# A Conformer macaron layer on one core: one more seven-product pair in each feed-forward group, four summed weight tiles a group, and the second feed-forward's two summed buffers exchanged

## The chip, the cores and the metric

The kernel runs on one core of a Trainium2 chip. The metric is the device time of one execution in microseconds, as the median of several runs. The core has a tensor engine (PE, with its weight loads shown as PEld), a vector engine (DVE), a scalar engine (ACT), GpSimd (POOL) and a sync engine (SP) that issues most of the transfers from HBM. Each engine works through its own list of instructions in a fixed order; an instruction whose inputs are not there waits, and so do those behind it on that engine.

## The reference, cut to what matters

```python
def swiglu_ffn(h, w_in, w_out):
    gate, up = jnp.split(h @ w_in, 2, axis=-1)
    return (jax.nn.silu(gate) * up) @ w_out

# per layer
h = rms_norm(x, ffn1_norm[l]);  x = x + 0.5 * swiglu_ffn(h, ffn1_w_in[l], ffn1_w_out[l])
...                             # convolution and gating mixers, output projection, cross-attention
h = rms_norm(x, ffn2_norm[l]);  x = x + 0.5 * swiglu_ffn(h, ffn2_w_in[l], ffn2_w_out[l])
return rms_norm(x, final_norm)
```

There are 256 tokens, the model's width is 2048 and the feed-forward's is 5632, so `w_in` is 2048 x 11264 and `w_out` 5632 x 2048, all in float32. The change touches the product with `ffn1_w_in` and, in one line, that with `ffn2_w_in`.

## The kernel before, in words

**Products in three parts.** A float32 number is split into a high part (ACT casts it, L397) and a low part (DVE subtracts the high part from it, L398). A product of two such numbers is high·high + high·low + low·high, three matrix products (`three`, L318 to L320; `by_two`, L331, L332 and L334). Each has a 128x128 stationary side and 512 columns. The weights pass through SBUF in tiles of 128 x 1024 (512 KB): SP loads the raw tile (L408), ACT makes its high part and DVE its low part, and PE uses both.

**Groups and pairs.** Each feed-forward's first product is done in 11 blocks j of 1024 columns (512 gate, 512 up). Block 0 is plain. In blocks 1 to 10, called groups, the 16 tiles k of a group are taken as 8 pairs, by the letters of PATTERNS. A "C" pair (`eight`) takes the eight products of two tiles as they are, 24 matrix products, and needs two splits. An "S" pair (`seven`) takes seven products of sums and differences, 21 matrix products; for it DVE makes the sums (L470, L471, L477, L484, 512 columns each) and three and a half tiles are split. The token side of an S pair is made once, by `sides`, beside block 0, into one of four places (`forms`), of which three are used.

**Summed tiles.** Some tiles of C pairs (SUMMED, k = 2, 7, 13) get their low part without DVE: SP loads the raw tile (L425), ACT writes its negative to the low half (L426) and its cast to the high half (L427), and POOL issues a transfer that loads the same weights again and adds them onto the low half (L428). There are two such buffers, `hl_s` and a part of `more` (in the second feed-forward `hl_s` and `hl_s2`), used by turns (`buffer`), with one raw tile each. The refill of a buffer is issued when the tile in it has been used (`following`): L426 then waits for the last product that reads the low half.

**The end of a group.** After the last S pair `joins_sevens` copies and adds sums (L521 on ACT, L522 to L525 on DVE); after the last pair DVE adds the remaining four banks (L550 four times), ACT takes the silu (L510) and DVE the product (L512). All eight PSUM banks are in use, so the first products of the next group wait for these adds.

**What sets the order.** The code is written in program order, and a scheduler at build time sorts the instructions onto the engines' lists; `issue_after` puts a part of the program behind a named instruction in that sorting. On the chip the lists are fixed. Raw tiles go round nine places (four of `wraw`, five of `spare`) less those given to summed tiles; split tiles go round three of `whl`, two of `ring` and one of `more`.

Of the kernel before, what the change touches and what calls it, by code (L numbers as in the profile page):

```python
# [2 lines left out]

# [1 line left out]

# [9 lines left out]
ALU = mybir.AluOpType  # L15
# [18 lines left out]
SCALE = float(HD) ** -0.5  # L34


PATTERNS = ("SCSCSCCC", "SCSCSCCC")

SUMMED = ((2, 7, 13), (2, 7, 13))
ALONE = (2, 10)  # L40


# [36 lines left out]
def layer(ctx: ExitStack, tc: tile.TileContext, a: dict):  # L79
    nc = tc.nc  # L80
    out = a["out"]
# [232 lines left out]
    NG = F // G  # L314
# [27 lines left out]
    class FeedForward:  # L342
# [4 lines left out]


        def __init__(self, stack, tags, x_hl, gain, w_in, pattern, summed, w_out=None, pair=False):
            self.w_out, self.out_forms = w_out, None  # L350
            self.x_hl, self.gain, self.w_in, self.pattern = x_hl, gain, w_in, pattern
            self.tags, self.pattern_sums = tags, summed
            self.spairs = [p for p, c in enumerate(pattern) if c == "S"]
            self.own = stack.enter_context(tc.tile_pool(name="own", bufs=1))
            self.low = ExitStack()
            low = self.low.enter_context(tc.tile_pool(name="h_low", bufs=1))
            self.high = ExitStack()
            high = self.high.enter_context(tc.tile_pool(name="h_high", bufs=1, side="right"))
# [12 lines left out]
            self.forms = [  # L371
                forms[:, i * 1024:(i + 1) * 1024].rearrange("p (f two n) -> p f two n", two=2, n=P) for i in range(4)
            ]
            spare = big.tile([P, 8192], F32, name="spare", tag=tags[2])
            self.x2 = spare[:, :4096].rearrange("p (t d) -> p t d", t=2)
            self.free = spare[:, 4096:]
            self.sums = spare[:, 4096:5120]
            self.raws = [spare[:, i * 1024:(i + 1) * 1024] for i in (5, 0, 1, 2, 3)]
            self.raw_at = 0

            self.raws_summed = [self.raws.pop()]
            self.u = [spare[:, 6144 + i * 512:6144 + (i + 1) * 512] for i in range(4)]
            self.at = 0
            self.next = None
            self.hA = self.hB = self.hC = None
            self.hls = [self.own.tile([P, 2, 1024], F32R, name="hl_s")]
            self.first = self.hls[0].rearrange("p a (f two n) -> p (a f) two n", f=2, two=2)
            if pair:
                self.hls.append(second)
                self.raws_summed.append(self.h[8].rearrange("p a b -> p (a b)"))  # L390
# [19 lines left out]

        def buffer(self, at):

            return at % 2 if not self.pair or self.sums_at[at][0] < 8 else 0

        def following(self, at):
            same = [i for i in range(at + 1, len(self.sums_at)) if self.buffer(i) == self.buffer(at)]
# [2 lines left out]
        def summed(self, at):  # L419

            if at >= len(self.sums_at):
                return
            j, k = self.sums_at[at]
            raw, hl = self.raws_summed[self.buffer(at)], self.hls[self.buffer(at)]
            nc.sync.dma_start(out=raw, in_=self.w_in[j, :, k])  # L425
            nc.scalar.activation(out=hl[:, 1], in_=raw, func=AF.Copy, scale=-1.0)  # L426
            nc.scalar.copy(out=hl[:, 0], in_=raw)  # L427
            nc.gpsimd.dma_start(out=hl[:, 1], in_=self.w_in[j, :, k], accum_op=ALU.add)  # L428
# [91 lines left out]
        def joins_sevens(self, b, p1, u2, u4, u5):  # L520
            nc.scalar.copy(out=p1, in_=b["1"])  # L521
            nc.vector.tensor_tensor(out=u2, in0=p1, in1=b["6"], op=ALU.add)  # L522
            nc.vector.tensor_tensor(out=u4, in0=u2, in1=b["5"], op=ALU.add)
            nc.vector.tensor_tensor(out=u2, in0=u2, in1=b["7"], op=ALU.add)
            nc.vector.tensor_tensor(out=u5, in0=u2, in1=b["5"], op=ALU.add)  # L525

        def group(self, j, r, after=()):
            if self.pair and j == NG - 2:
                both = self.high_pool.tile([P, 2, 2, G], F32, name="h_pair", tag="pair")
                self.h[NG - 2:] = [both[:, i] for i in range(2)]  # L530
            b = {}
            self.begun = set()
            self.banks(b, "57612348")
            after = list(after)
            p1, u2, u4, u5 = self.u
            n = len(self.pattern)
            for p, c in enumerate(self.pattern):
                if c == "S":
                    self.seven(j, p, b, p == self.spairs[-1])
                    if p == self.spairs[-1]:  # L540
                        self.joins_sevens(b, p1, u2, u4, u5)
                else:
                    late = p > self.spairs[-1] and len(after) > 0
                    self.eight(j, p, b, p == n - 1, late)
                    if p > self.spairs[-1] + 1:
                        for _ in range(2):
                            if after:
                                after.pop(0)()
            for acc, u in (("2", p1), ("4", u2), ("3", u4), ("8", u5)):
                nc.vector.tensor_tensor(out=u, in0=u, in1=b[acc], op=ALU.add)  # L550
            self.give(j, (p1, u2), (u4, u5), r)
# [58 lines left out]
        def run(self, before, after, root, more=None, early=False):  # L610
            acc = token_accs()
            sums = self.pattern_sums
            self.sums_at = [(j, k) for j in range(1, NG) for k in sums if j < NG - 1 or k < min(14, sums[-1])]
            if self.pair:

                self.sums_at = [at for at in self.sums_at if at[0] < 8] + [(j, k) for j in range(8, NG) for k in ALONE]
            for k in range(KD):
                if k == 0 and early:
                    w = self.early(before)
                else:  # L620
                    before(k)
# [68 lines left out]
    with ExitStack() as stack:  # L690
        ff = FeedForward(stack, ("S1", "S0", "S2"), x_hl, lambda k: gains[:, k:k + 1], a["ffn1_w_in"], PATTERNS[0], SUMMED[0], a["ffn1_w_out"])
# [6 lines left out]
        def x_more(k):  # L698
            if k == 6:
                nc.sync.dma_start(out=pv, in_=a["pv"])  # L700
            if k in (2, 4, 6, 8):
                x_squares(k // 2 - 1)
            if k in (6, 9, 12):
                ff.sides(k // 3 - 2)

        def x_root():
            nc.vector.tensor_tensor(out=r_x, in0=tot[:, 0], in1=tot[:, 1], op=ALU.add)
# [3 lines left out]
        def x_given():  # L711

            more = xt.tile([P, 4, 1024], F32R, name="more", tag="x")
            ff.ring.append(more[:, :2])
            ff.hls.append(more[:, 2:])
            ff.raws_summed.append(ff.raws.pop())

        turns = ff.run(x_arrives, x_more, x_root, x_given, early=True)

# [81 lines left out]
    with ExitStack() as stack:  # L801
        with tc.tile_pool(name="mix", bufs=1) as pool:
# [239 lines left out]
            at = [part for _, part in later].index(conv_swish_0)  # L1042
# [327 lines left out]
```

## Time and profile before

| | before |
|---|---|
| median of the runs, us | 2088.95 (2088.29 to 2089.9) |
| time of the profiled execution, us | 2088.91 |
| its span in the trace, us | 2087.1 |
| PE matrix products in the trace | 9765 |
| DVE, ACT, POOL instructions in the trace | 2302, 1470, 81 |
| HBM read, MB | 437.44 |

The span runs from the first to the last instruction in the trace. The time of an execution is 1.8 us longer, which lies around the span.

### The profile page before, as it was taken

How to read it: one execution, taken by the hardware profiler on the slowest of the kernel's cores; microseconds unless marked ns; L12 is line 12 of the kernel's file. 1: busy time of each engine (PE TensorE's matmuls, PEld its weight loads, DVE VectorE, ACT ScalarE, POOL GpSimd, SP SyncE). 2: the span in 40 equal slices, each digit the busy share in tenths (PEclk: the TensorE clock that was granted, in tenths of full speed). 3: DMA queues.
4: the chain of work that ended last, by engine and by line, in shares of the span. 5: the costliest groups of instructions: out<-in, count | busy, mean ns of one | idle time of the engine just before them, and what ended most of it. 6: DMA issues, size and time to landing. Idle time of an engine off the chain costs nothing.

```text
span 2087.1 us, 26730 instructions
## 1 busy us (share of the span) xinstructions
PE 2076.4 (99%) x9765; PEld 1739.0 (83%) x9765; DVE 1622.5 (78%) x2302; ACT 1174.4 (56%) x1470; POOL 66.0 (3%) x81
## 2 busy tenths in 40 slices
PE   9999999999999999999999999999999999999998
PEld 8888888888888888888888899888888888888886
DVE  7888888877777689989877666778888888787754
ACT  8665666555545554445764455566665655554443
POOL 0000000000000000000000000000000000000000
PEclk9999999999999999999999999999999999999999
DMA  9787778755566576655555543687777777556664
GB/s 366 246 263 246 232 223 263 230 182 192 188 203 234 180 238 199 186 179 187 180 196 192 184 160 124 200 291 224 237 236 253 222 217 230 169 166 203 195 192 152
DMA packets 122245, 441.30 MB, mean 211 GB/s; under 512 B 13569, under 2 KB 13953, under 8 KB 121729
## 3 DMA queue, kind: packets, MB, share of 16 engines
q1 hardware_dynamic: 113184, 407.08, 57.1%
q0 software_dynamic: 8352, 31.46, 8.1%
q8 instruction: 76, 1.25, 0.2%
q10 hardware_dynamic: 576, 1.06, 0.1%
q14 instruction: 57, 0.46, 0.1%
HBM read 437.44 MB, written 2.10 MB: 211 GB/s over the span
## 4 chain that ended last, share of the span: by engine, by line
PE 87%; issue 11%; POOL 1%; DMA 1%; ACT 0%; DVE 0%; DVEq 0%; POOLq 0%
PE acc L332 11%; PE acc L331 11%; PE acc L334 11%; PE acc L204 8%; PE acc L205 8%; PE acc L203 8%; PE acc L154 8%; PE acc L162 4%; PE acc L318 3%; PE acc L319 3%; PE acc L320 3%; PE aux L306 1%; PE aux L318 1%; PE aux L319 1%; PE aux L320 1%
## 5 line engine op out<-in xcount | busy, mean ns | idle before, releaser
L124 ACT CAST hl<-raw 128x1024 fp32r<-128x1024 f32 (+1 forms) x315 | 327.1, 1040 | 358.9 <-PE acc L205 191.9
L125 DVE TENSOR_TENSOR hl<-raw,hl 128x1024 fp32r<-128x1024 f32 (+1 forms) x315 | 381.2, 1212 | 165.0 <-ACT hl L124 163.6
L397 ACT CAST hl<-raw 128x1024 fp32r<-128x1024 f32 (+1 forms) x151 | 147.6, 988 | 117.3 <-PE acc L334 48.2
L398 DVE TENSOR_TENSOR hl<-raw,hl 128x1024 fp32r<-128x1024 f32 (+1 forms) x151 | 172.2, 1145 | 47.4 <-ACT hl L397 45.7
L398 DVE TENSOR_TENSOR hl<-spare,hl 128x1024 fp32r<-128x1024 f32 (+1 forms) x125 | 144.7, 1162 | 32.5 <-ACT hl L397 30.3
L397 ACT CAST hl<-spare 128x1024 fp32r<-128x1024 f32 (+1 forms) x125 | 124.3, 1002 | 66.4 <-PE acc L334 24.2
L332 PE MATMUL acc<-hl,x_hl 128*128 128x512 f32 x388 | 140.9, 390 | 0.1
L331 PE MATMUL acc<-hl,x_hl 128*128 128x512 f32 x388 | 135.7, 390 | 0.0
L334 PE MATMUL acc<-hl,x_hl 128*128 128x512 f32 x388 | 120.6, 390 | 0.0
L397 ACT CAST ring<-spare 128x1024 fp32r<-128x1024 f32 (+1 forms) x83 | 82.1, 993 | 59.6 <-issue 19.1
L398 DVE TENSOR_TENSOR ring<-spare,ring 128x1024 fp32r<-128x1024 f32 (+1 forms) x83 | 95.2, 1150 | 20.3 <-ACT ring L397 19.6
L332 PE MATMUL acc<-ring,x_hl 128*128 128x512 f32 x276 | 101.3, 389 | 0.0
L204 PE MATMUL acc<-hl,x_hl 128*128 128x512 f32 x256 | 100.7, 393 | 0.0
L204 PE MATMUL acc<-hl,m_hl 128*128 128x512 f32 x256 | 100.4, 392 | 0.0
L205 PE MATMUL acc<-hl,m_hl 128*128 128x512 f32 x256 | 100.3, 392 | 0.0
L205 PE MATMUL acc<-hl,x_hl 128*128 128x512 f32 x256 | 100.0, 391 | 0.0
L331 PE MATMUL acc<-ring,x_hl 128*128 128x512 f32 x276 | 98.6, 390 | 0.0
L203 PE MATMUL acc<-hl,m_hl 128*128 128x512 f32 x256 | 90.9, 392 | 0.0
L203 PE MATMUL acc<-hl,x_hl 128*128 128x512 f32 x256 | 90.2, 392 | 0.0
L334 PE MATMUL acc<-ring,x_hl 128*128 128x512 f32 x276 | 86.2, 389 | 0.0
L332 PEld LDWEIGHTS acc<-hl,x_hl 128*128 128x128 f32 x388 | 72.6, 188 | 15.5 <-DVE hl L133 0.4
L334 PEld LDWEIGHTS acc<-hl,x_hl 128*128 128x128 f32 x388 | 72.9, 188 | 15.1
(518 smaller groups left out, 5100.8 us busy)
## 6 DMA issues: line engine op xcount, KB each, us to landing
spare<-in_ffn_w_in SPq DMA_DIRECT2D x184, 512.0 KB, 6.8
raw<-in_ffn_w_in SPq DMA_DIRECT2D x157, 512.0 KB, 5.9
raw<-in_ffn_w_out SPq DMA_DIRECT2D x138, 512.0 KB, 4.0
hl_s<-in_ffn_w_in POOLq DMA_DIRECT2D x42, 512.0 KB, 8.3
raw<-in_w_mix_vg SPq DMA_DIRECT2D x32, 512.0 KB, 4.3
raw<-in_w_k SPq DMA_DIRECT2D x32, 512.0 KB, 3.6
raw<-in_w_v SPq DMA_DIRECT2D x32, 512.0 KB, 4.0
raw<-in_w_mix_out SPq DMA_DIRECT2D x32, 512.0 KB, 4.4
```

The lines of the kernel that those rows point to most:

```text
L124: nc.scalar.copy(out=hl[:, 0, :size], in_=raw[:, :size])
L125: newest[0] = nc.vector.tensor_tensor(out=hl[:, 1, :size], in0=raw[:, :size], in1=hl[:, 0, :size].bitcast(F32), op=ALU.subtract)
L154: done = nc.tensor.matmul(acc, lhsT=hi[:, k], rhs=xs[k], start=first and k == 0, stop=last and k == kk - 1, skip_group_check=True,)
L162: done = nc.tensor.matmul(acc[:, 0], lhsT=lo[:, k], rhs=xs[k][:, 0], start=False, stop=last and k == kk - 1, skip_group_check=True,)
L203: nc.tensor.matmul(acc[t], lhsT=x[:, 0, s], rhs=hi[:, k], start=k0 + k == 0, stop=False)
L204: nc.tensor.matmul(acc[t], lhsT=x[:, 0, s], rhs=lo[:, k], start=False, stop=False)
L205: nc.tensor.matmul(acc[t], lhsT=x[:, 1, s], rhs=hi[:, k], start=False, stop=k0 + k == nk - 1)
L331: nc.tensor.matmul(acc[t][g], lhsT=x[:, 0, s], rhs=hi[:, cols[g]], start=(t, g) in first, stop=False)
L332: nc.tensor.matmul(acc[t][g], lhsT=x[:, 0, s], rhs=lo[:, cols[g]], start=False, stop=False)
L334: nc.tensor.matmul(acc[t][g], lhsT=x[:, 1, s], rhs=hi[:, cols[g]], start=False, stop=last)
L397: self.cast = nc.scalar.copy(out=hl[:, 0, :n], in_=raw[:, :n])
L398: newest[0] = nc.vector.tensor_tensor(out=hl[:, 1, :n], in0=raw[:, :n], in1=hl[:, 0, :n].bitcast(F32), op=ALU.subtract)
```

## The change

In the first feed-forward, groups 1 to 9 take the pattern SCSCSCSC, with four S pairs; group 10 keeps SCSCSCCC. The summed tiles are k = 2, 6, 10 and 14 (in group 10 those below 13), so four a group instead of three, still in two buffers, but with three raw tiles by turns instead of two; the third is taken from the ring of raw tiles. `sides` is called four times in block 0 instead of three. The first S pair of a group is sorted in behind the last add of `joins_sevens` of the group before. In the second feed-forward the two summed buffers exchange their turns for j < 8, and what comes after stays in `hl_s`. Lines move by two to nine.

```diff
-PATTERNS = ("SCSCSCCC", "SCSCSCCC")
-SUMMED = ((2, 7, 13), (2, 7, 13))
+PATTERNS = ("SCSCSCSC", "SCSCSCCC")
+LAST = "SCSCSCCC"
+SUMMED = ((2, 6, 10, 14), (2, 7, 13))
...
         def buffer(self, at):
-            return at % 2 if not self.pair or self.sums_at[at][0] < 8 else 0
+            if self.pair:
+                return (at + 1) % 2 if self.sums_at[at][0] < 8 else 0
+            return at % 2
...
-            raw, hl = self.raws_summed[self.buffer(at)], self.hls[self.buffer(at)]
+            raw = self.raws_summed[self.buffer(at) if self.pair else at % len(self.raws_summed)]
+            hl = self.hls[self.buffer(at)]
...
-            nc.vector.tensor_tensor(out=u5, in0=u2, in1=b["5"], op=ALU.add)
+            self.joined = nc.vector.tensor_tensor(out=u5, in0=u2, in1=b["5"], op=ALU.add)
...
-            n = len(self.pattern)
-            for p, c in enumerate(self.pattern):
+            pattern = self.pattern if j < NG - 1 else LAST
+            n, done = len(pattern), pattern.rindex("S")
+            for p, c in enumerate(pattern):
                 if c == "S":
-                    self.seven(j, p, b, p == self.spairs[-1])
-                    if p == self.spairs[-1]:
+                    with nullcontext() if p or self.joined is None else tc.issue_after(self.joined.ins):
+                        self.seven(j, p, b, p == done)
+                    if p == done:
                         self.joins_sevens(b, p1, u2, u4, u5)
...
-            self.sums_at = [(j, k) for j in range(1, NG) for k in sums if j < NG - 1 or k < min(14, sums[-1])]
+            self.sums_at = [(j, k) for j in range(1, NG) for k in sums if j < NG - 1 or k < 13]
...
-            if k in (6, 9, 12):
-                ff.sides(k // 3 - 2)
+            if k in (4, 7, 10, 13):
+                ff.sides(k // 3 - 1)
...
-            ff.raws_summed.append(ff.raws.pop())
+            ff.raws_summed += [ff.raws.pop() for _ in range(2)]
```

Over the whole program PE has 9701 rows in its list where it had 9728, DVE 2353 for 2304, ACT 1487 for 1456 and POOL 96 for 86 (ten more adding transfers); SP has 788 in both. The rows below are from the lists: line, operation, out<-in, size. The number behind a name tells buffers apart; two names can be one place in turn.

**First place: from block 0 to group 1, on ACT.** `h0` is the result of block 0 (silu, L510 before, L516 now), `spare` and `raw` are raw tiles. Before:

```order
L397 CAST hl_471<-spare_132 128x1024
L397 CAST hl_526<-raw_505 128x1024
L397 CAST more_490<-raw_503 128x1024
L397 CAST ring_131<-spare_132 128x1024
L510 ACT_TABLE_LOAD
L510 ACTIVATE h0_120<-acc_134,r_x2_109 128x512
L397 CAST hl_536<-raw_505 128x512
L510 ACTIVATE h0_120<-acc_136,r_x2_109 128x512
```

Now, with the first S pair of group 1 in `hl_532`, `ring_131` (the sums) and `more_498`:

```order
L399 CAST ring_131<-spare_132 128x1024
L399 CAST hl_479<-spare_132 128x1024
L516 ACT_TABLE_LOAD
L516 ACTIVATE h0_120<-acc_134,r_x2_109 128x512
L516 ACTIVATE h0_120<-acc_136,r_x2_109 128x512
L399 CAST hl_532<-spare_132 128x1024
L399 CAST ring_131<-spare_132 128x1024
L399 CAST more_498<-spare_132 128x1024
L432 ACTIVATE more_498<-spare_132 128x1024
```

The three casts of the first S pair stood ahead of the table load and the two silu rows, and stand behind them. PE's list at this place now reads as follows; `acc_136` and `acc_137` are block 0's banks, and the L320 rows are the first products of group 1:

```order
L333 MATMUL acc_137<-hl_479,x_hl_108 128x512
L334 MATMUL acc_137<-hl_479,x_hl_108 128x512
L336 MATMUL acc_136<-hl_479,x_hl_108 128x512
L336 MATMUL acc_137<-hl_479,x_hl_108 128x512
L320 MATMUL acc_503<-ring_131 128x512
L320 MATMUL aux_504<-ring_131 128x512
L320 MATMUL aux_505<-more_498,ring_131 128x512
L320 MATMUL acc_506<-more_498,x_hl_108 128x512
```

The silu of `acc_136` follows the last but one row of block 0, and the first row of group 1 needs `ring_131`, two casts behind that silu.

**Second place: from group 2 to group 3, on ACT.** L521 (now L527) is the copy of `joins_sevens`; `h2` is the result of group 2. Before, the group's last refill of a summed tile (L426) stands at the end:

```order
L521 COPY spare_132<-acc_793 128x512
L397 CAST ring_131<-spare_132 128x1024
L397 CAST more_490<-spare_132 128x1024
L397 CAST hl_1099<-spare_132 128x1024
L397 CAST hl_1109<-raw_1093 128x1024
L397 CAST hl_1118<-raw_1095 128x1024
L426 ACTIVATE more_490<-spare_132 128x1024
```

Now:

```order
L527 COPY spare_132<-acc_808 128x512
L399 CAST ring_131<-spare_132 128x1024
L432 ACTIVATE more_498<-spare_132 128x1024
L433 CAST more_498<-spare_132 128x1024
L399 CAST hl_1121<-spare_132 128x1024
L399 CAST hl_1167<-raw_1165 128x1024
L399 CAST ring_131<-spare_132 128x1024
L516 ACTIVATE h2_122<-spare_132,r_x2_109 128x512
```

`hl_1121` is the sums' tile of group 3's first S pair and the `ring_131` below it the second one of that pair. They stood ahead of the refill and stand behind it. In PE's list the last row that reads the low half which L432 overwrites (an L334 row of tile k = 14) stands 14 rows ahead of the first row of group 3; the row that needs `hl_1121` is that first row, and the one that needs `ring_131` is two rows on.

**Third place: refills inside a group, on ACT.** This is group 3's refill of `hl_s` after k = 2 (for k = 10), in the list now:

```order
L399 CAST hl_1192<-spare_132 128x1024
L399 CAST hl_1202<-raw_1186 128x1024
L399 CAST ring_131<-raw_1188 128x1024
L399 CAST more_498<-raw_1237 128x1024
L432 ACTIVATE hl_s_133<-spare_132 128x1024
L433 CAST hl_s_133<-spare_132 128x1024
```

The two casts ahead of L432 wait for PE rows that stand four and two rows ahead of the one L432 waits for. From that row, the last that reads the old low half, to the first that needs the new one, PE's list has 41 rows. Counted in this way, the distances in groups 1 to 10 of the first feed-forward were 106 to 115 rows; now they are 40 to 81, and six of them are 40, 41, 41, 45, 40 and 41 rows (in groups 2, 3, 6, 6, 8 and 9; the 45 is that of `more`, the others are of `hl_s`). In the second feed-forward one distance was 43 rows and the others 72 and more; now the least is 72.

More of the change, by code (lines that the diff above doesn't have):

```diff
@@ L1 @@
 from collections import deque
-from contextlib import ExitStack
+from contextlib import ExitStack, nullcontext
 import numpy as np
@@ L383, in __init__ @@
             self.at = 0
-            self.next = None
+            self.next = self.joined = None
             self.hA = self.hB = self.hC = None
@@ L535, in group @@
             p1, u2, u4, u5 = self.u
-            n = len(self.pattern)
-            for p, c in enumerate(self.pattern):
+            pattern = self.pattern if j < NG - 1 else LAST
+            n, done = len(pattern), pattern.rindex("S")
+            for p, c in enumerate(pattern):
                 if c == "S":
-                    self.seven(j, p, b, p == self.spairs[-1])
-                    if p == self.spairs[-1]:
+                    with nullcontext() if p or self.joined is None else tc.issue_after(self.joined.ins):
+                        self.seven(j, p, b, p == done)
+                    if p == done:
                         self.joins_sevens(b, p1, u2, u4, u5)
                 else:
-                    late = p > self.spairs[-1] and len(after) > 0
+                    late = p > done and len(after) > 0
                     self.eight(j, p, b, p == n - 1, late)
-                    if p > self.spairs[-1] + 1:
+                    if p > done + 1:
                         for _ in range(2):
```

## The prediction

> **What bounds the kernel now.** I read the page first, then what PE waits for, then the stretches of one group, then the rows of single places. The page's head, busy line, PE clock by slices and chain:
>
> ```profile
> span 2087.1 us, 26730 instructions
> ...
> PE 2076.4 (99%) x9765; PEld 1739.0 (83%) x9765; DVE 1622.5 (78%) x2302; ACT 1174.4 (56%) x1470; POOL 66.0 (3%) x81
> ...
> PEclk9999999999999999999999999999999999999999
> ...
> PE 87%; issue 11%; POOL 1%; DMA 1%; ACT 0%; DVE 0%; DVEq 0%; POOLq 0%
> ```
>
> PE is busy 99% of the span at full clock, and the chain that ended last is made of PE rows. The view of PE's waits has two entries:
>
> ```profile
> PE aux L232 <- DVE ones L229: 1.1, 1, 1.1
> PE acc L332 <- DMA hl_s<-in_ffn_w_in: 0.8, 1, 0.8
> ```
>
> So a product less is time less, and each new wait of PE is time more. The second entry, in the second feed-forward, and the rows around it are the most useful of the trace. PE's timeline there, eleven microseconds earlier:
>
> ```profile
> 1695.75 0.39 PE L331 MATMUL acc<-hl_s,x_hl 128*128 128x512 f32 x1
> 1695.98 0.39 PE L332 MATMUL acc<-hl_s,x_hl 128*128 128x512 f32 x1
> 1696.20 0.39 PE L331 MATMUL acc<-hl_s,x_hl 128*128 128x512 f32 x1
> 1696.43 0.39 PE L332 MATMUL acc<-hl_s,x_hl 128*128 128x512 f32 x1
> ```
>
> The timelines of ACT and POOL:
>
> ```profile
> 1696.86 1.06 ACT L426 ACTIVATE hl_s<-spare 128x1024 fp32r<-128x1024 f32 x1 [1.21 <-PE acc L332]
> ...
> 1698.32 0.86 POOL L428 DMA_DIRECT2D hl_s<-in_ffn_w_in  x1 [27.69 <-ACT hl_s L426]
> ```
>
> The chain's piece, start and length:
>
> ```profile
> 1698.32 8.77 DMA hl_s<-in_ffn_w_in
> ```
>
> And PE's timeline at its end (in brackets the wait and what ended it):
>
> ```profile
> 1705.95 0.39 PE L331 MATMUL acc<-hl_s,x_hl 128*128 128x512 f32 x1
> 1707.13 0.50 PE L332 MATMUL acc<-hl_s,x_hl 128*128 128x512 f32 x1 [0.80 <-DMA hl_s<-in_ffn_w_in]
> 1707.47 0.39 PE L334 MATMUL acc<-hl_s,x_hl 128*128 128x512 f32 x1
> ```
>
> Three things are read from these rows. PE rows start every 0.227 us ((1696.43 - 1695.75) / 3), though each is shown as 0.39 long. A refill goes: last reader at 1696.43, ACT 0.43 later, POOL's transfer 1.46 after that, landing 8.77 later, PE 0.04 later, in all 10.70 us. And 43 rows were left for it, 9.75 us, so PE was held: 1705.95 to 1707.13 and then 0.34 where rows take 0.227, **1.07 us** too long. That is the one hold of PE in either feed-forward's groups.
>
> The stretches of block 0 and of two plain groups (columns: PE, PEld, DVE, ACT, POOL busy us and counts, clock, share of the DMA engines, GB/s):
>
> ```profile
> 5.00:46.00 41.00, 40.93 (x184) 33.64 (x183) 35.19 (x60) 35.33 (x56) 1.02 (x1) 1.00 1.03 392
> 131.00:172.00 41.00, 41.00 (x182) 33.99 (x181) 34.36 (x41) 24.84 (x28) 2.50 (x3) 1.00 0.76 244
> 214.00:255.00 41.00, 41.00 (x183) 33.96 (x182) 34.33 (x41) 25.56 (x29) 2.60 (x3) 1.00 0.78 244
> ```
>
> In a group PE has no gap, DVE 6.7 us to spare in 41 and ACT 16; shares of busy time alone would let the change pass. What decides is who stands behind whom.
>
> **The change part by part.** The sum starts from the profiled execution, 2088.91 us (span 2087.1, 1.8 around it), within 0.1 us of the median of the runs, 2088.95.
>
> *Removed.* PE's list has 27 rows less (three in each of nine groups): 27 x 0.227 = **-6.1 us**. The exchange of buffers in the second feed-forward takes the 43-row refill away; the least distance there is then 72 rows, 16.3 us, for a need of 10.7: **-1.07 us**. Free of all else the kernel would take 2081.7.
>
> *Added work.* DVE has 49 rows more, 5.4 a group; at the 0.69 to 1.22 us of its rows (shown below) that is 3.7 to 6.6 us a group on top of 34.4. The period is 4 x 21 + 4 x 24 = 180 PE rows, 40.8 us (183 before). It just fits, so as busy time I cost it at nothing; at the upper end it would be 0.2 us a group. The fourth `sides` stands in block 0, where DMA is full (1.03 of the engines) but DVE and ACT have 5.7 us: nothing, at most 0.5. The ring of raw tiles shrinks from seven to six places, for 12 loads a group where there were 13: a place comes round every 6 x 40.8 / 12 = 20.4 us instead of 7 x 41.5 / 13 = 22.3. Plain loads land in 6.2 (median, below), so I cost it at nothing.
>
> *First place, start of group 1.* ACT's rows there before, timeline:
>
> ```profile
> 47.99 1.28 ACT L510 ACT_TABLE_LOAD   x1
> 49.29 0.69 ACT L510 ACTIVATE h<-acc,r_x 128x512 f32<-128x512 f32 x1
> 49.87 0.61 ACT L397 CAST hl<-raw 128x512 fp32r<-128x512 f32 x1
> ...
> 50.96 1.05 ACT L397 CAST hl<-spare 128x1024 fp32r<-128x1024 f32 x1
> 51.91 1.05 ACT L397 CAST more<-spare 128x1024 fp32r<-128x1024 f32 x1
> ```
>
> A silu row holds ACT 0.58, a cast 0.95, and its result is there after 1.05. Now the second silu waits for PE's last but one row of block 0, 0.45 ahead of group 1. It starts at -0.45 + 0.43 = -0.02, the casts follow at 0.56, 1.51 and 2.46, and the third ends at 3.51. PE's third row of group 1, due at 0.45, needs it: 3.51 + 0.05 - 0.45 = **+3.1 us**. Before, these casts stood ahead of the silu and nothing was held. Bounds: if the raw tiles come late too (DMA is full there), 5; if they are early, 3.1 stays, since the silu sets it.
>
> *Second place, nine group starts.* L432 waits for the last reader of k = 14's low half, 12 to 15 rows ahead of the next group, and the casts of that group's first S pair stand behind it. From group 2 to 3: the reader at 0, L432 at 0.43, L433, two casts, and the third cast after four rows of 0.96 at 4.27, ready at 5.32 + 0.05; PE wants it 16 rows on, at 3.63: held 1.74. The nine starts have their own number of casts in between and of rows ahead; worked out in the same way they give 1.0, 1.7, 0.5, 1.3, 1.5, 0.7, 1.0, 1.7 and 0.5, together **+10.0 us**. In three of them DVE's subtraction for the low part is late as well, behind the adds L550, which end last here:
>
> ```profile
> 130.97 0.69 DVE L550 TENSOR_TENSOR spare<-spare,acc 128x512 f32<-128x512 f32 x1 [1.53 <-PE acc L334]
> 131.57 1.22 DVE L398 TENSOR_TENSOR ring<-raw,ring 128x1024 fp32r<-128x1024 f32 x1
> 132.71 1.88 DVE L550 TENSOR_TENSOR spare<-spare,acc 128x512 f32<-128x512 f32 x3
> ```
>
> Three splits at 1.14 with the adds at 0.60 between them stand against four PE rows (0.91) from one to the next: 0.8 us each, **+2.5 us**, between 0 and 4. Before, those casts stood ahead of the refill, and PE was not held. With a lag on ACT of 0.23 instead of 0.43 the nine would still give 8.
>
> *Third place, refills inside a group.* The view of DMA issues from 90 to 420 us (the queue of the adding transfers: packets, MB, share of the DMA engines; and the plain loads of `spare`, with the median to landing), then the landings of `hl_s` and of `more` from 46 to 463 us:
>
> ```profile
> q0 software_dynamic: 3410, 12.40, 21.2%
> ...
> spare<-in_ffn_w_in SPq DMA_DIRECT2D x67, 512.0 KB, 6.2
> ```
>
> ```profile
> DMA to landing us min/median/max: 6.7/8.7/9.3
> ```
>
> ```profile
> DMA to landing us min/median/max: 6.7/8.5/10.0
> ```
>
> With 106 to 115 rows (24 us and more) these landings never held PE. Six are left 40, 41, 41, 45, 40 and 41 rows: 9.07, 9.29, 9.29, 10.20, 9.07, 9.29 us. They need 0.43, then 0.5 (one cast ahead of L432, waiting for a PE row two before) or 1.0 (two casts), 1.46, 8.6 and 0.04: 11.0 or 11.5. Held: 2.0, 2.2, 2.2, 0.8, 2.0, 2.2 = **+11.4 us**. The one refill of before with so few rows is the one that held PE, which is why I trust this term. Of the landing I take 8.6, between the medians; at 6.7, the least, 1 us is left, at 9.3 15.6.
>
> At this place the Trainium skill ("DMA: Bandwidth & Descriptors", Anatomy of one DMA — SWDGE (gpsimd) path) gives for a transfer from GpSimd about 2.0 us and its bytes at 436 GB/s, which would be an estimate of 3.2 us for these 512 KB; by that no refill would hold PE, and the sum would be 11.4 less. The trace disagrees, 8.77 for the one that held PE.
>
> **The sum.** 2088.9 - 6.1 - 1.1 + 3.1 + 10.0 + 2.5 + 11.4 = 2108.7; I forecast **2109 us**, 1.0% slower.
>
> **Rivals.**
>
> *Not slower: ScalarE's waiting rows do not hold the rows behind them.* Then the casts run when their tiles are there: the first two places and the three splits vanish, and the refills lose their 0.5 to 1.0 ahead of L432, which leaves 1.5 + 1.2 + 1.2 + 0.3 + 1.5 + 1.2 = 6.9. That is 2081.7 + 6.9 = 2088.6, no change, and faster down to 2082 if they also land in 7. It decides from the point where the first cast starts before L432. For it speaks only that busy time has room. Against it, ACT's timeline in a group:
>
> ```profile
> 85.18 1.06 ACT L426 ACTIVATE hl_s<-spare 128x1024 fp32r<-128x1024 f32 x1 [3.93 <-PE acc L332]
> 86.15 1.04 ACT L427 CAST hl_s<-spare 128x1024 fp32r<-128x1024 f32 x1
> 87.09 0.61 ACT L397 CAST hl<-raw 128x512 fp32r<-128x512 f32 x1
> ```
>
> ACT stood 3.93 us ahead of a waiting L426 and took nothing from behind it. The Trainium skill ("Perfetto Trace Analysis", Tensor Engine Instruction) calls ACT's queue strictly first in, first out; by that this rival falls, and the trace agrees with its 3.93. Chance 0.08, half of it for no change.
>
> *Refills land fast,* in 6.7, because held PE leaves the queues emptier: 2108.7 - 10.4 = 2098. Chance 0.15. Against it: the queue of these transfers carries a third more per group, and the DMA engines' share was 0.76 to 0.78.
>
> *Transfers land late.* q0 carries a third more per group, 28% for 21.2%, beside loads that do not shrink. If the adding transfers take 10.0, the most seen, the six refills add 1.4 each (8.4), and four more of 48 rows, 10.9 us, which need 12 then, about 0.5 each where no held start lies between: 2118. Chance 0.17.
>
> *The change doesn't do what it says:* the lists show the 27 rows gone, so it can't; the summed buffers of the second feed-forward are at 72 rows and more there too.
>
> *PE's clock drops.* The trace has no wait of PE above 1.1 us, and the clock is 1.00 in its stretches. The Trainium skill ("TensorE: Matmul & The Clock Gate", Part 1: The HAM clock gate) halves the clock after an idle window of about 3.4 us, which no run here shows. At half clock for as long, 15 rows would take 3.4 us more; only the first place, at 3.1, comes near: 2112. Chance 0.03.
>
> **How the numbers follow.** The forecast's own mechanism has 0.57. The range is that sum with its bounds (first place 3 to 5, second 8 to 14 with the splits, third 1 to 15.6) and the two rivals beside it: 2096 to 2119, which leaves out the first rival's 0.08 and a tenth at the ends. A measurement can tell about 0.2% (4 us) from no change. Faster by more 0.06 (half of the first rival, and errors in several terms at once), within it 0.06, slower 0.88.
>
> **What would show it.** Right: ACT's L432 of k = 14 idle for PE, and PE's waits listing L320 <- ACT casts about ten times, 0.5 to 1.7 each, one near 50 us of 3 us, and L334 <- DMA about six times near 2 us; PE 9701 products; nothing at the old 1705.95. Wrong: PE's busy share again 99% with only the start's wait (first rival); waits of PE for DMA well above 2 us, or more than ten of them (transfers late); a clock below 1 near 50 us.

## The result, and the profile after

The changed kernel takes **2115.42 us** (median of 4 runs, 2115.0 to 2117.12), before 2089.39 on the same chip: a ratio of 1.0127, 95% interval 1.0114 to 1.0139. It is 26 us slower. The forecast was 2109 with a range of 2096 to 2119. The profiled execution took 2115.0 us. The head of its page, with the busy line and the chain:

```profile
span 2113.2 us, 26712 instructions
...
PE 2083.4 (99%) x9738; PEld 1731.7 (82%) x9738; DVE 1649.1 (78%) x2351; ACT 1191.5 (56%) x1501; POOL 74.8 (4%) x91
...
PE 82%; issue 14%; DVE 1%; POOL 1%; DMA 0%; ACT 0%; POOLq 0%; DVEq 0%; ACTq 0%
```

PE has its 27 products less (9738 for 9765 in the trace; the 9701 of the prediction counts the list) and is still busy 99%; a reader of shares would see nothing. The view of PE's waits (us in total, times, longest) had two entries before and has twelve now, of which these are the first six:

```profile
PE acc L334 <- DMA hl_s<-in_ffn_w_in: 6.2, 5, 1.8
PE aux L320 <- ACT ring L399: 3.5, 3, 1.2
PE acc L320 <- ACT ring L399: 2.4, 1, 2.4
PE acc L334 <- DMA more<-in_ffn_w_in: 2.0, 2, 1.3
PE aux L320 <- ACT more L399: 1.8, 4, 1.1
PE acc L321 <- DVE hl L400: 1.6, 2, 1.1
```

The old wait of the second feed-forward is gone. **First place**, the start of group 1, timelines of ACT and of PE:

```profile
49.88 0.69 ACT L516 ACTIVATE h<-acc,r_x 128x512 f32<-128x512 f32 x1 [0.44 <-PE acc L336]
50.47 1.03 ACT L399 CAST hl<-spare 128x1024 fp32r<-128x1024 f32 x1
51.41 1.04 ACT L399 CAST ring<-spare 128x1024 fp32r<-128x1024 f32 x1
52.35 1.05 ACT L399 CAST more<-spare 128x1024 fp32r<-128x1024 f32 x1
```

```profile
49.46 0.61 PE L336 MATMUL acc<-hl,x_hl 128*128 128x512 f32 x2
52.50 0.50 PE L320 MATMUL acc<-ring 128*128 128x512 f32 x1 [2.43 <-ACT ring L399]
52.84 0.40 PE L320 MATMUL aux<-ring 128*128 128x512 f32 x1
53.45 0.50 PE L320 MATMUL aux<-more,ring 128*128 128x512 f32 x1 [0.22 <-ACT more L399]
```

The silu starts 0.42 after block 0's last but one PE row, and three casts follow; PE starts as soon as the second and the third are there. **Second place**, from group 2 to group 3, ACT and PE:

```profile
137.61 1.06 ACT L432 ACTIVATE more<-spare 128x1024 fp32r<-128x1024 f32 x1 [4.84 <-PE acc L334]
138.58 1.03 ACT L433 CAST more<-spare 128x1024 fp32r<-128x1024 f32 x1
139.51 1.04 ACT L399 CAST hl<-spare 128x1024 fp32r<-128x1024 f32 x1
140.46 1.04 ACT L399 CAST hl<-raw 128x1024 fp32r<-128x1024 f32 x1
141.41 1.04 ACT L399 CAST ring<-spare 128x1024 fp32r<-128x1024 f32 x1
```

```profile
137.19 0.39 PE L334 MATMUL acc<-more,x_hl 128*128 128x512 f32 x1
...
140.94 0.40 PE L320 MATMUL aux<-hl,ring 128*128 128x512 f32 x1
142.50 0.50 PE L320 MATMUL aux<-ring 128*128 128x512 f32 x1 [1.16 <-ACT ring L399]
```

L432 starts 0.42 after its reader at 137.19, having stood idle for 4.84 us with the casts behind it; the first of them, of the sums, had its tile from 136.71 on, when DVE's second sum was done. The fifth row of the chain ends at 142.45, where PE takes it. **Third place**, the refill of `hl_s` in group 3, whose last reader ran at 151.93; ACT, POOL and PE:

```profile
153.40 1.06 ACT L432 ACTIVATE hl_s<-spare 128x1024 fp32r<-128x1024 f32 x1
...
154.86 0.87 POOL L434 DMA_DIRECT2D hl_s<-in_ffn_w_in  x1 [14.92 <-ACT hl_s L432]
...
161.71 0.50 PE L334 MATMUL acc<-hl_s,x_hl 128*128 128x512 f32 x1 [0.32 <-DMA hl_s<-in_ffn_w_in]
```

From reader to L432 it takes 1.47 (1.43 foretold), from there to POOL 1.46, and to PE 6.85 (8.6 was taken). A fourth kind was not foreseen: a refill with 54 rows to go (12.2 us) that starts late. DVE, ACT and PE in group 2:

```profile
119.60 0.69 DVE L477 TENSOR_TENSOR spare<-raw 128x512 f32<-128x512 f32 x1 [3.54 <-DMA raw<-in_ffn_w_in]
120.21 0.68 DVE L490 TENSOR_TENSOR spare<-spare 128x512 f32<-128x512 f32 x1
```

```profile
121.01 0.62 ACT L399 CAST hl<-spare 128x512 fp32r<-128x512 f32 x1 [7.26 <-PE acc L336]
121.53 1.05 ACT L399 CAST hl<-raw 128x1024 fp32r<-128x1024 f32 x1
122.49 1.05 ACT L432 ACTIVATE more<-spare 128x1024 fp32r<-128x1024 f32 x1
```

```profile
133.38 0.50 PE L334 MATMUL acc<-more,x_hl 128*128 128x512 f32 x1 [1.34 <-DMA more<-in_ffn_w_in]
```

DVE waited 3.54 us for a raw tile; the tile that ACT casts at 121.01 is made behind it, by L490, and is there at 120.89. (The bracket names a PE row, which by this profile ended a few hundredths after that.) L432 stands two rows further on and starts 2.4 us later than its own reader (119.62) would let it.

Where the 26.1 us of the span went, from the starts of PE's rows, each interval against 0.227:

| | forecast | measured |
|---|---|---|
| 27 products | -6.1 | -6.1 |
| the second feed-forward's refill | -1.1 | -1.1 |
| start of group 1 | +3.1 | +3.2 |
| casts at nine group starts | +10.0 | +11.3 |
| splits at three of them | +2.5 | +2.7 |
| refills inside groups | +11.4 | +10.6 |
| PE at half clock | 0 | +1.6 |
| first output block | 0 | +2.5 |
| block 0 and rows of a few hundredths | 0 | +1.4 |

### The profile page after: what moved, and what is told of

Its sections match the earlier page's. It is cut to its first block, busy times and chain, and to the rows that moved or that the text cites. A ratio compares the mean times of both kernels' runs of the same rounds, so it can differ in the third digit from the quotient of the medians.

```text
span 2113.2 us, 26712 instructions
## 1 busy us (share of the span) xinstructions
PE 2083.4 (99%) x9738; PEld 1731.7 (82%) x9738; DVE 1649.1 (78%) x2351; ACT 1191.5 (56%) x1501; POOL 74.8 (4%) x91
## 4 chain that ended last, share of the span: by engine, by line
PE 82%; issue 14%; DVE 1%; POOL 1%; DMA 0%; ACT 0%; POOLq 0%; DVEq 0%; ACTq 0%
PE acc L334 10%; PE acc L336 10%; PE acc L333 10%; PE acc L206 8%; PE acc L207 8%; PE acc L205 8%; PE acc L156 8%; PE acc L164 4%; PE acc L321 2%; PE acc L322 2%; PE acc L320 2%; PE aux L308 1%; PE aux L320 1%; PE aux L321 1%; PE aux L322 1%
## 5 line engine op out<-in xcount | busy, mean ns | idle before, releaser
L126 ACT CAST hl<-raw 128x1024 fp32r<-128x1024 f32 (+1 forms) x315 | 327.3, 1041 | 355.1 <-PE acc L207 192.2
L127 DVE TENSOR_TENSOR hl<-raw,hl 128x1024 fp32r<-128x1024 f32 (+1 forms) x315 | 380.9, 1211 | 163.8 <-ACT hl L126 162.4
L400 DVE TENSOR_TENSOR hl<-raw,hl 128x1024 fp32r<-128x1024 f32 (+1 forms) x163 | 185.1, 1139 | 59.3 <-ACT hl L399 58.3
L399 ACT CAST hl<-raw 128x1024 fp32r<-128x1024 f32 (+1 forms) x163 | 158.6, 985 | 104.5 <-PE acc L336 54.3
L399 ACT CAST hl<-spare 128x1024 fp32r<-128x1024 f32 (+1 forms) x120 | 118.8, 1003 | 77.7 <-DVE spare L477 33.1
L400 DVE TENSOR_TENSOR hl<-spare,hl 128x1024 fp32r<-128x1024 f32 (+1 forms) x120 | 138.2, 1163 | 23.3 <-ACT hl L399 22.7
L334 PE MATMUL acc<-hl,x_hl 128*128 128x512 f32 x340 | 121.0, 390 | 0.0
L333 PE MATMUL acc<-hl,x_hl 128*128 128x512 f32 x340 | 117.3, 391 | 0.0
L400 DVE TENSOR_TENSOR ring<-spare,ring 128x1024 fp32r<-128x1024 f32 (+1 forms) x85 | 96.1, 1132 | 16.9 <-ACT ring L399 16.4
L336 PE MATMUL acc<-hl,x_hl 128*128 128x512 f32 x340 | 106.5, 389 | 0.0
L206 PE MATMUL acc<-hl,x_hl 128*128 128x512 f32 x256 | 100.7, 393 | 0.0
L207 PE MATMUL acc<-hl,x_hl 128*128 128x512 f32 x256 | 99.9, 390 | 0.0
L400 DVE TENSOR_TENSOR ring<-raw,ring 128x1024 fp32r<-128x1024 f32 (+1 forms) x67 | 74.6, 1117 | 22.9 <-ACT ring L399 22.6
L205 PE MATMUL acc<-hl,x_hl 128*128 128x512 f32 x256 | 90.5, 392 | 0.0
L399 ACT CAST ring<-raw 128x1024 fp32r<-128x1024 f32 (+1 forms) x67 | 64.5, 967 | 40.8 <-PE acc L322 17.3
L434 POOL DMA_DIRECT2D hl_s<-in_ffn_w_in x47 | 41.2, 876 | 1203.5 <-ACT hl_s L432 618.4
L334 PE MATMUL acc<-ring,x_hl 128*128 128x512 f32 x228 | 80.5, 390 | 0.0
L334 PE MATMUL acc<-hl_s,x_hl 128*128 128x512 f32 x188 | 73.8, 393 | 6.3 <-DMA hl_s<-in_ffn_w_in 6.2
```

The lines of the kernel that those rows point to most:

```text
L126: nc.scalar.copy(out=hl[:, 0, :size], in_=raw[:, :size])
L127: newest[0] = nc.vector.tensor_tensor(out=hl[:, 1, :size], in0=raw[:, :size], in1=hl[:, 0, :size].bitcast(F32), op=ALU.subtract)
L205: nc.tensor.matmul(acc[t], lhsT=x[:, 0, s], rhs=hi[:, k], start=k0 + k == 0, stop=False)
L206: nc.tensor.matmul(acc[t], lhsT=x[:, 0, s], rhs=lo[:, k], start=False, stop=False)
L207: nc.tensor.matmul(acc[t], lhsT=x[:, 1, s], rhs=hi[:, k], start=False, stop=k0 + k == nk - 1)
L333: nc.tensor.matmul(acc[t][g], lhsT=x[:, 0, s], rhs=hi[:, cols[g]], start=(t, g) in first, stop=False)
```

## The experiments

Each diff is against the changed kernel, except where said. Beside these runs the kernel before measured 2089.5 to 2089.8. "Held" is PE's time above 0.227 a row from the end of block 0 to the first rows of group 10, worked out in the same way as for the table, and good to some 0.2 us; the change has 29.4. It is read from the one profiled execution of each run.

**Without issue_after** (label e1_no_issue_after).

```diff
-                    with nullcontext() if p or self.joined is None else tc.issue_after(self.joined.ins):
+                    with nullcontext():
```

> The change without its issue_after on the last add of joins_sevens; all else as in the change. In the lists the casts of a group's first S pair then stand ahead of the refill of the tile k = 14 again, and the distances between the last reader of a summed tile and the first reader of its refill are 48 rows and more (they were 40 to 45 six times). Theory (who stands behind whom): the nine group starts lose 11.3 us of waits on casts and 2.7 on splits, the refills lose 10.6 but for one of 48 rows (about 1 us), and the 1.6 us at half clock go; the first place (3.2) stays. 2115.4 - 25.2 = 2090 us, between 2088 and 2093. Rival 1 (load: DVE, DMA or the shrunken ring of raw tiles are the bound, the waits only show where it surfaces): the work is the same, so the waits come back elsewhere, 2105 us and more. Rival 2 (half): the casts go but the refills stay long, since the buffers are still used four times a group: 2102 us.

Measured 2110.94 us, ratio 1.0099 (1.0083 to 1.0114), held 25.7. My theory's 2090 was missed by 21 us, and the number of rival 1 was the nearer. The theory's mechanism did what was said, since the waits on refills and on the first pair's casts are down to 0.2 each (the 2.4 is the first place), but another wait stands in their place. PE's waits:

```profile
PE aux L320 <- DVE spare L530: 9.8, 4, 3.4
PE acc L320 <- ACT ring L399: 2.4, 1, 2.4
PE acc L320 <- DVE spare L559: 1.9, 3, 1.5
...
PE acc L334 <- DMA more<-in_ffn_w_in: 0.2, 1, 0.2
```

DVE's timeline at the start of group 3, where PE waited from 138.06 to 140.29:

```profile
133.10 0.69 DVE L476 TENSOR_TENSOR spare<-raw 128x512 f32<-128x512 f32 x1 [1.27 <-DMA raw<-in_ffn_w_in]
134.28 0.69 DVE L477 TENSOR_TENSOR spare<-raw 128x512 f32<-128x512 f32 x1 [0.48 <-DMA raw<-in_ffn_w_in]
134.89 0.68 DVE L528 TENSOR_TENSOR spare<-spare,aux 128x512 f32<-128x512 f32 x1
...
139.56 0.68 DVE L530 TENSOR_TENSOR spare<-spare,aux 128x512 f32<-128x512 f32 x1
```

DVE stands at the sums of group 3's second S pair, whose raw tiles are not there, with the adds that free PE's banks behind and between that pair's rows. So issue_after takes away one wait and brings another of about the same size. In the run without it some 7 us of the 25.7 were lost by rows at half clock.

**Two raw tiles, the ring of raw tiles at seven places** (label e2_two_raws).

```diff
-            raw = self.raws_summed[self.buffer(at) if self.pair else at % len(self.raws_summed)]
+            raw = self.raws_summed[self.buffer(at)]
...
-            ff.raws_summed += [ff.raws.pop() for _ in range(2)]
+            ff.raws_summed.append(ff.raws.pop())
```

> The change, with issue_after, but with two raw tiles for the summed tiles by turns of the buffer, as before, so that the ring of raw tiles keeps seven places. Theory: at the start of group 1 the raw tiles of the first S pair come from places that are free earlier, the lists have its casts ahead of the two silu rows, and the wait of 3.2 us near 50 us goes; the group starts and the refills stay: 2110 to 2114 us. Rival (the place of the silu alone makes the first wait, whatever the raw tiles): the wait near 50 us stays and the time is 2115. Rival (the ring of six places costs time all along): 2105 or less, with fewer waits of DVE on raw tiles inside the groups.

Measured 2111.77 us (1.0103, 1.0086 to 1.012), held 27.5. The wait near 50 us is gone: PE's first row of group 1 starts at 49.73, 0.23 after block 0's last. The first place comes from which raw tiles the first S pair gets, and not from the silu alone. The rest stays, with some 6 us lost at half clock, for 1.6 in the change.

**Both edits** (label e3_no_issue_after_two_raws).

> Both edits together: no issue_after, two raw tiles. What is left of the change are the fourth S pair, the four summed tiles, the fourth call of sides and the exchanged buffers. Theory: without the waits at the group starts, in the refills and at the start of group 1, the 6.1 us of products and the 1.1 us of the second feed-forward are kept but for some 1 to 2 us in groups and about 2.5 us in the first output block: 2084 to 2088 us, faster than before. Rival (load): 2100 and more.

Measured 2091.45 us (1.0009, 0.9999 to 1.0018), held 6.2: not the 2084 to 2088 of the theory, and far from the rival's 2100. PE's waits for L530 are down from 9.8 us to 2.9. The two edits are worth 24 us together and some 4 each alone: with six places the wait moves from ACT to DVE, with issue_after it is on ACT whatever the places.

**The kernel before with the exchanged buffers alone** (label e4_swap_alone; against before).

```diff
-            return at % 2 if not self.pair or self.sums_at[at][0] < 8 else 0
+            if self.pair:
+                return (at + 1) % 2 if self.sums_at[at][0] < 8 else 0
+            return at % 2
```

> The kernel before with only the exchange of the two summed buffers of the second feed-forward. Theory: the one wait of PE for a refill there (43 rows) goes and nothing else moves: 1.07 us less, 2088.3 us against 2089.4 of the same chip's kernel before, and no wait of PE on hl_s in the trace. Rival (the wait moves to another refill of that feed-forward): the same time and another wait of about 1 us.

Measured 2088.10 us (0.9993, 0.9984 to 1.0002). The interval has 1 in it, but the trace shows the wait gone and PE's rows 1.09 us earlier from there on.

**Other summed tiles, two raw tiles, no issue_after** (label e5_other_tiles; on top of both edits).

```diff
-SUMMED = ((2, 6, 10, 14), (2, 7, 13))
+SUMMED = ((2, 7, 11, 15), (2, 7, 13))
```

> No issue_after, two raw tiles, and the summed tiles k = 2, 7, 11, 15 instead of 2, 6, 10, 14 (in group 10 those below 13). The number of products and of summed tiles is the change's. In the lists the least distance from the last reader of a summed tile to the first reader of its refill is 58 rows (13.2 us, need 10.7), the casts of a group's first S pair stand ahead of the last refill, and the copy and adds of joins_sevens have fewer rows ahead of them. Theory (who stands behind whom): the 5.4 us of waits that the run with two raw tiles and without issue_after still has in the groups fall below 2, the first output block keeps its 2.5 us: 2085 to 2087 us against 2089.8 for before. Rival (a fourth S pair brings DVE or the DMA queues to their limit in each group): PE waits 4 us and more in the groups and the time is 2088 to 2092, however the tiles are chosen.

Measured **2084.49 us** (0.9977, 0.9968 to 0.9987), held 0.2: faster than before, as expected and a little below. All of PE's waits:

```profile
PE aux L234 <- DVE ones L231: 1.1, 1, 1.1
PE acc L321 <- DVE hl L400: 1.1, 1, 1.1
PE acc L334 <- DVE hl L135: 0.2, 1, 0.2
PE acc L334 <- DVE hl L400: 0.2, 1, 0.2
```

Two of its stretches in the groups (columns as in the prediction):

```profile
131.00:172.00 41.00, 41.00 (x182) 33.95 (x181) 39.40 (x51) 28.37 (x32) 3.49 (x4) 1.00 0.89 262
214.00:255.00 41.00, 41.00 (x182) 33.97 (x181) 37.78 (x48) 28.90 (x33) 3.61 (x5) 1.00 0.86 260
```

PE without a gap beside DVE at 39.4 of 41 and DMA at 0.89: the fourth S pair and the fourth summed tile fit. Load was not the cause.

**The same with the turn of split tiles moved** (label e6_other_tiles_and_turn; on top of it).

```diff
-        ff.ring, ff.raws = [], [raws[:, q] for q in range(4)]
+        ff.ring, ff.raws = [], [raws[:, q] for q in range(4)]; ff.at += 2
```

> The same, and at the start of the first output block the turn of the split tiles is set on by two (ff.at += 2). The change has moved that turn, since it makes 215 split tiles before that block where there were 207; theory: the waits of PE in the output block near 540 us (0.2, 1.2 and 0.3 us with their late starts, 2.5 us together, not there in the kernel before) come from it and go: 2.0 to 2.5 us less than the run without this edit, 2083 to 2085 us. Rival: they come from the later or busier DMA queues or from the six or seven places of raw tiles, and stay: no difference between the two runs.

Measured 2083.91 us (0.9973, 0.9963 to 0.9983). The first output block's time above 0.227 a row falls from 3.6 to 2.3 us (before 1.3), but 1.1 come back in the second one, so half of the theory holds and the times of the two runs can't be told apart. It is the fastest kernel here, 5.6 us below before.

**issue_after with those tiles and two raw tiles** (label e7_issue_after_other_tiles).

> Two raw tiles and summed tiles 2, 7, 11, 15, but with issue_after as in the change. In the lists three refills have 41 and 49 rows, the others 58 and more, and the first S pair's casts stand behind joins_sevens's adds. Theory: what issue_after costs is its place in the lists, with any choice of tiles: one or two refills with waits of 1 to 2 us, and splits of the first S pair behind the adds L559 at several starts, 8 to 16 us more than the run without it: 2094 to 2102. Rival (only the tile k = 14 was at fault, since its refill stands at the end of the group): within 2 us of the run without issue_after.

Measured 2102.6 us (1.0063, 1.0048 to 1.0078), held 15.8: 18 us more than without it. The tile k = 14 was not the cause alone. PE now waits for splits (L400, 5.8 us in eight waits, one of them, 1.1, in the first output block) and casts (1.9); its wait for refills is 0.2, though one has 41 rows.

**Three raw tiles with those tiles, no issue_after** (label e8_three_raws_other_tiles).

> No issue_after, summed tiles 2, 7, 11, 15, but three raw tiles for them as in the change, so six places in the ring of raw tiles. All refills have 64 rows and more. Theory (the ring of six): DVE's first rows of an S pair wait for their raw tiles with the adds of joins_sevens behind them, so PE's first rows of a group wait for DVE L530, L531 or L559, 1 to 3 us at most starts: 2103 to 2112. Rival (the waits without issue_after came from the choice of tiles): as the run with two raw tiles, 2085 to 2087.

Measured 2125.78 us (1.0174, 1.0159 to 1.0189), held 38.5: the theory's direction and waits, but 41 us more than with two raw tiles where the theory had 16 to 27. PE's first entry and DVE's first two waits for DMA (9.2 and 9.6 us for the same two with two raw tiles, in e5_other_tiles):

```profile
PE acc L320 <- DVE spare L559: 12.2, 6, 2.6
...
DVE spare L477 <- DMA spare<-in_ffn_w_in: 42.1, 20, 3.6
DVE spare L476 <- DMA spare<-in_ffn_w_in: 22.2, 13, 3.0
```

**issue_after on the second S pair** (label e9_issue_after_second_pair).

```diff
-                    with nullcontext() if p or self.joined is None else tc.issue_after(self.joined.ins):
+                    with nullcontext() if p != 2 or self.joined is None else tc.issue_after(self.joined.ins):
```

> The change with one character of its condition turned: issue_after now holds back the second S pair of a group (p == 2) instead of the first (p == 0). Three raw tiles and the tiles 2, 6, 10, 14 as in the change. In the lists the first S pair's casts stand ahead of the refill of k = 14, the adds of joins_sevens stand ahead of the second pair's rows, and four refills still have 42 to 45 rows. Theory: the wrong pair was held back. The 14.0 us at the group starts go, without the waits for L530 that the run without any issue_after had; the four short refills keep about 1 us each, the start of group 1 its 3.2 and the output block its 2.5: 2092 to 2096 us. Rival 1 (any issue_after there costs 10 us): 2105 and more. Rival 2 (six places of raw tiles make the adds or casts late, whichever pair is held): waits of PE for DVE L530 or L559 of 10 us in all, 2103 and more.

Measured 2093.41 us (1.0018, 1.0009 to 1.0027), held 6.2: 22 us less than the change, within the theory's range, with all its other parts kept. PE's waits:

```profile
PE acc L320 <- ACT ring L399: 2.4, 1, 2.4
...
PE acc L334 <- DMA more<-in_ffn_w_in: 1.0, 1, 1.0
PE acc L334 <- DMA hl_s<-in_ffn_w_in: 0.5, 1, 0.5
PE aux L320 <- DVE spare L530: 0.4, 1, 0.4
```

The first place is left, the casts are in time, and L530 too. Of the four refills with 42 to 45 rows two held PE. The profiled execution, 2090.86, is the quickest of ten that go up to 2096.2; what held the others is not in the trace.

**The same with two raw tiles** (label e11_second_pair_two_raws) **and with two raw tiles, other tiles and the turn** (label e10_second_pair_two_raws_tiles_turn).

> issue_after on the second S pair and two raw tiles, the tiles 2, 6, 10, 14 as in the change. Refills of 42, 42, 49, 49 and 49 rows. Theory: against the run with three raw tiles the start of group 1 loses its 3.2 us, the rest stays: 2088 to 2092; the difference to the run with tiles 2, 7, 11, 15 (least refill 56 rows) is what short refills cost, 2 to 5 us with the 2.5 of the output block apart. Rival (short refills do not matter once the casts are in time): 2085 to 2087.

> issue_after on the second S pair, two raw tiles, tiles 2, 7, 11, 15, and the turn of the split tiles set on by two before the output block. The least refill has 56 rows. Theory: nothing is left to wait for in the groups; 6.1 and 1.1 us are kept: 2082.5 to 2084.5 us, at or below the same without issue_after (2083.9). Rival (holding back the second pair makes its casts late now and then): 2085 to 2088.

Measured 2089.67 us (1.0, 0.9991 to 1.0009), held 4.1, and 2086.12 us (0.9983, 0.9974 to 0.9992), held 1.3 (its profiled execution, 2084.26, is the quickest of eleven). The first is as expected; the second lies in the range of its rival. With all in place, holding back the second pair gains nothing over holding back none.

## Why the prediction was right, and where it was not

**Right, by its own steps.** The method of the second place, counting the rows of ACT's list behind a row whose start is tied to PE, gave the nine starts as 1.0, 1.7, 0.5, 1.3, 1.5, 0.7, 1.0, 1.7, 0.5; measured 1.1, 1.8, 0.6, 1.4, 1.5, 1.4, 1.1, 1.8, 0.6. Only group 7's, 1.4 for 0.7, is off, for a reason that was not looked into. The first place, 3.1, came out at 3.2, and the two gains as forecast. Undoing parts shows each: two raw tiles remove the first place, issue_after on another pair removes the second, the exchange alone removes the wait of the second feed-forward. The first rival, ScalarE letting rows pass a waiting one, is refuted by L432's 4.84 us of idling, the last 0.9 of them with a ready cast behind it. By the Trainium skill ("Perfetto Trace Analysis", Tensor Engine Instruction) ACT's queue is first in, first out, and the trace agrees.

**The third place was right in sum and wrong in its parts.** I gave 11.4 us to six refills of 40 to 45 rows. They held PE 6.0: 2.0, 0.6, 0.4, 0, 2.1 and 1.0. The step that failed for them is the landing of 8.6, taken for all alike; from POOL's row to PE's, the five that held PE took 8.6, 6.9, 6.6, 8.6 and 7.3. The other 4.6 us come from three refills of 48 to 54 rows (in groups 2, 3 and 5), which the forecast put at nothing. Their L432 started 2.9, 1.1 and 3.0 us after its reader, where 0.43 is possible, behind casts of a pair whose raw tile DVE had waited 3.5, 2.5 and 1.5 us for; and they took 9.4, 9.2 and 9.6 from POOL to PE. With starts at 0.43 and these landings some 0.2 of the 4.6 us would be left, by an estimate from the same rows. That the two errors come to nearly the same, 10.6 for 11.4, is luck.

So the other wrong step is "Plain loads land in 6.2, so I cost it at nothing": a late raw tile has a price where a refill stands behind it on ACT. By the median the adding transfers did not land later (8.4 for 8.7 in `hl_s`), but single raw tiles did, 11.9 us at most where it was 9.7. That the ring of six made them late is not shown: with seven places (the run with two raw tiles) one took 12.2, and DVE waited up to 2.8. Nor is a late tile enough: DVE waited up to 2.9 us for raw tiles before, and up to 3.1 with issue_after on the second pair, and there refills held PE little or not at all.

The run with three raw tiles and the other summed tiles shows what the third one can cost, 41 us against the same with two. Landing times don't explain it: those of `spare` from 90 to 420 us have a median of 7.0 and a longest of 10.0, with two raw tiles 6.8 and 10.3. How much of that is the ring itself and how much the order that the scheduler made from it was not separated.

**The term that was missing** is the first output block, 2.5 us. The fourth S pair changes how many split tiles have been made before it, 215 for 207, and so where the turn of the split tiles stands. Moving the turn took 1.3 of it away there. The rest is open.

**The reason given for the slowdown was too short.** I read the casts behind the refill as the price of the change. The run without issue_after shows that the wait had been moved from another place: without it the adds of `joins_sevens` are late by as much. The run with issue_after on the second pair shows that it was put on the wrong pair. The pair whose raw tiles DVE waits for, with the adds behind, is the second.

**The rival of the clock,** given 0.03 at the first place, took place elsewhere at half its price: 3.4 us at half clock cost 1.6, and not the 3.4 that I had, since only 8 rows fall into them, not 15. PE's timeline there, and two stretches around it (clock in the column ahead of the DMA share):

```profile
381.27 0.50 PE L334 MATMUL acc<-hl_s,x_hl 128*128 128x512 f32 x1 [1.80 <-DMA hl_s<-in_ffn_w_in]
...
382.31 0.63 PE L333 MATMUL acc<-more,x_hl 128*128 128x512 f32 x1
382.74 0.63 PE L334 MATMUL acc<-more,x_hl 128*128 128x512 f32 x1
```

```profile
379.00:382.00 3.00, 1.20 (x6) 0.69 (x5) 0.00 (x0) 0.00 (x0) 0.00 (x0) 1.00 0.99 370
382.00:386.00 4.00, 4.00 (x12) 3.08 (x12) 3.29 (x5) 2.30 (x3) 0.00 (x0) 0.57 0.38 124
```

One microsecond after a hold of 2 us that ended at 381.27, PE's rows come every 0.43 us, from 382.31 to 385.72. The Trainium skill ("TensorE: Matmul & The Clock Gate", Part 1: The HAM clock gate) puts this behind an idle window of about 3.4 us. The trace differs: PE's longest wait in it is 2.4 us, and the one here 1.80.

## What to carry to other kernels

When a change reorders the lists, read for each row that waits for PE what stands behind it on its engine, and multiply; that found some 23 of the 33 us that PE was held here, where busy shares said that all fits. A wait that an ordering rule removes can be moved to the next engine, as here, so look at what the rule was there for before undoing it: here the rule on another pair, or a buffer given back, kept the gain. A buffer taken from a ring of loads is not free, even if a place still comes round far more slowly than a load lands (20.4 us for 6.2 here): neither the median landing nor the longest told what it would cost, so look at what stands behind the rows that wait for the raw tiles, or try it.

## What the runs showed of the hardware

A row of PE that has been held costs 0.11 us more than its wait: the interval to the next row is 0.34 instead of 0.227 (52.50 to 52.84, 140.61 to 140.94). In the changed kernel that is some 4 us of the 29.4 held.

PE's clock halved for about 3.4 us after some holds of near 2 us and above, but not after each: the 2.0 us ending at 381.27 were followed by it, 1.9 us ending at 254.48 and 2.6 ending at 52.50 were not, and in the run without issue_after the same 2.6 us at the start of group 1 were. A long hold isn't needed: in the run with two raw tiles the granted clock is 0.57 from 226 to 230, after holds of 0.7 and 1.2 us that ended at 223.73 and 225.53. With the longest hold, 3.6 us ending at 398.88 in the run without issue_after, it lasted longer: the rows after it are slow for 5.5 us, from 399.5 on. What decides is not settled here.
